# A decoder block on one core: weight tiles all at one place within 512 bytes, 64 bytes past four token operands and level with three

## The chip, the core and the metric

The kernel runs on one core of one Trainium2 chip. The metric is the device time of one execution in microseconds (us): 2169.51 us for the kernel before, the median of three runs (2157.59, 2169.51 and 2170.23).

## The reference, cut to what matters

One layer of a hybrid decoder block on 512 tokens of width 2048, all in float32. First comes token mixing (gated linear attention and differential softmax attention side by side, with one input and one output projection), then a gated MLP with a short causal convolution on its gate branch. Each part has a norm before and a norm after it and is added to the residual.

```python
def conv_ffn(h, w_ffn_in, conv_w, conv_b, w_ffn_out):
    up = h @ w_ffn_in                      # 512x2048 @ 2048x11264
    a, b = up[..., :D_FF], up[..., D_FF:]  # D_FF = 5632
    a = ...                                # causal convolution of width 3, plus conv_b
    return (jax.nn.gelu(a, approximate=True) * b) @ w_ffn_out

def reference(x, ...):
    h = rmsnorm(x, attn_pre_norm[l])
    m = token_mixer(h, ...)                # ends with  o @ w_o
    x = x + rmsnorm(m, attn_post_norm[l])
    h = rmsnorm(x, ffn_pre_norm[l])
    f = conv_ffn(h, ...)
    x = x + rmsnorm(f, ffn_post_norm[l])
```

## The kernel before, in words

**Arithmetic.** Every large product is made of three matmuls. A value is split into a high part, which ScalarE writes (L130 for weights), and a low part, the rest, which VectorE writes (L131); the three products are high by high, low by high and high by low. A weight tile ("granule") has 128 partitions by 1024 values. It is loaded into `raw` or `rt` and split into the tiles `whi` and `wlo`, of which the pool `w` has three buffers each. Tokens that were split lie in the two large tiles `ah` and `al`.

**Stages.** The input projections and the attention come first. The output projection `w_o` follows, with `evac_m` (L625 to L629) taking each finished bank: ScalarE squares it for the norm (L627, its output goes to a scratch tile `jk5`), VectorE multiplies it by the gain (L629). `to_ffn`, whose order is written by hand, turns the result into tokens for the MLP; there the matmuls of the first weights of `w_ffn_in` run on 256 tokens at a time with weights in spare tiles `xhi` and `xlo`, or in `whi` and `wlo`. Then comes the **up stage**: 20 units (ten groups of columns, two branches), each a seven-product scheme in place of eight block products. The class `Unit` runs the seven segments x0, z0, y0, z1, x1, y1, y2. A segment takes two granules. Its token operand is one of a11, a12, a22, s7, which are quarters of `ah` and `al`, or one of the three sums s5, s2, s3, which have tiles of their own (`s5h`, `s5l` and so on). In `up_prods` (L920 to L922) a matmul streams 256 tokens, two blocks of 128 values, against 128 by 128 weights: 24 matmuls a granule, 48 a segment, 336 a unit. When a group is done, `token_sums` makes the sums of its results for the stage after, in VectorE additions (L988) into tiles of tag `sum`, each stored to DRAM by a DMA that SyncE issues. Last comes the **down stage** with the same scheme: in `down_prods` (L1017 to L1019) a matmul streams 512 weight columns against 128 by 128 tokens.

**Places in SBUF.** The tile framework gives the addresses. In the built program `ah`, `al`, the six tiles of the sums, and `xhi` and `xlo` all start at 256 modulo 512 bytes, and every block of 128 values that a matmul reads of them starts there too. A buffer of `whi` or `wlo` is `GR + 64` values long, 4352 bytes, which is eight and a half times 512, so that neighbouring buffers alternate: `whi` starts at 256, 0, 256 modulo 512 and `wlo` at 0, 256, 0. Where `place_w[0]` is 16, the 1024 values begin 16 values (64 bytes) into the buffer, at 320 or 64. That is so in all segments of the up stage, where `self.a == 4`, and for the `whi` and `wlo` of `w_ffn_in` in `to_ffn`. Elsewhere it is 0. The matmul's stationary operand is loaded by its own instruction (LDWEIGHTS, PEld in the profile), which runs while the matmul before it still streams.

**Order.** Outside of the parts ordered by hand, the framework's scheduler sets each engine's order, and each engine takes its instructions in that order. A tile that is taken from a pool waits until the last use of the buffer's earlier tile is over, its DMA included.

Of the kernel before, what the change touches and what calls it, by code (L numbers as in the profile page):

```python
# [9 lines left out]
F32 = mybir.dt.float32  # L10
F32R = mybir.dt.float32r
U8 = mybir.dt.uint8
AF = mybir.ActivationFunctionType
# [4 lines left out]
P = 128  # L18
# [12 lines left out]
GR = 1024  # L31
# [4 lines left out]
def hybrid_layer(ctx: ExitStack, tc: tile.TileContext, x, attn_pre_norm, w_in, w_alpha_up, b_alpha,  # L36
# [10 lines left out]
    def dma(o, i):  # L47
        return nc.sync.dma_start(out=o, in_=i)
# [3 lines left out]
    act = nc.scalar.activation  # L52
# [22 lines left out]
    wpool = ctx.enter_context(tc.tile_pool(name="w", bufs=3))  # L75
# [30 lines left out]
    place_w = [0]  # L106

    def halves():
        sl = slice(place_w[0], place_w[0] + GR)
        return [wpool.tile([P, GR + 64], F32R, name=n, tag=n)[:, sl] for n in ("whi", "wlo")]  # L110

    kept = []

# [7 lines left out]
    def granule(src, a, raw=None, spare=None, hl=None):  # L121
        if raw is None:
            raw = load(src, a)
        if hl is not None:
            hi, lo = hl[:, 0, :], hl[:, 1, :]
        elif spare:
            hi, lo = spare_halves(spare)
        else:
            hi, lo = halves()
        act(hi, raw, AF.Copy)  # L130
        tt(lo, raw, hi.bitcast(F32), ALU.subtract)  # L131
        r = "p (a b) -> p a b"
        return hi.rearrange(r, a=a), lo.rearrange(r, a=a)
# [182 lines left out]
    for li, hs in enumerate(LEVELS):  # L316
        nb = 64 // hs
        m = setup[:, 1024 + 64 * li:1024 + 64 * (li + 1)]
# [298 lines left out]
    wp = wo.enter_context(tc.tile_pool(name="wo", bufs=1))  # L617
    m = [wp.tile([P, D], F32, name=f"m{t}") for t in range(NT)]
# [4 lines left out]
    ssm = [few.tile([P, 4], F32, name=f"ssm{t}") for t in range(NT)]  # L623

    def evac_m(c, t, b):  # L625
        jk = wp.tile([P, 512], F32, name="jk5", tag="jk5", bufs=1)
        act(jk, b, AF.Square, accum_out=ssm[t][:, c:c + 1])  # L627
        sl = slice(512 * c, 512 * (c + 1))
        tt(m[t][:, sl], b, g1[:, sl], ALU.mult)  # L629

    order = [(s + 8) % 16 for s in range(KT)]
    for c in range(3):
        proj_n(w_o3, 512 * c, lambda t, b, c=c: evac_m(c, t, b), order)
# [3 lines left out]
    def to_ffn():  # L637
# [10 lines left out]
        def evac(t):  # L648
            xr[t] = wp.tile([P, D], F32, name="xr", tag="xr", bufs=2)
            dma(xr[t], x2[t * P:(t + 1) * P, :])  # L650
            evac_m(3, t, banks[t])
            ss = small.tile([P, 1], F32, name="ss", tag="ss")
            nc.vector.reduce_sum(ss, ssm[t], axis=AX.X)
            rs[t] = rsqrt_mean(ss, D)
# [94 lines left out]
    fp = ctx.enter_context(tc.tile_pool(name="fp", bufs=2))  # L749
# [102 lines left out]
    class Unit:  # L852
# [4 lines left out]
        def run(self, seg, op, raws):  # L857
            c = seg[0]
            if seg[1] == "0":
                self.banks[c] = self.chain(c)  # L860
            for g in range(2):
                turn[0] += 1
                place_w[0] = 16 if self.a == 4 else 0
                hl = granule(None, self.a, raws[g], spare=extra[0] and turn[0] % 4 == 0)
                self.prods(self.banks[c], op, g, hl, seg[1] == "0")

# [111 lines left out]
    def token_sums(gi, u0, u1):  # L978
        c, i = (gi - 1) // 2, (gi - 1) % 2
        T = [slice(0, 256), slice(256, 512)]  # L980
        a11, a21, a12, a22 = u0[:, :, T[0]], u0[:, :, T[1]], u1[:, :, T[0]], u1[:, :, T[1]]

        def put(n, src):
            dma(sd[c][n][:, i, :].rearrange("p (n t) -> p n t", n=2), src)

        def add(n, x, y, op):
            t = fp.tile([P, 2, 256], F32, name=n, tag="sum", bufs=3)
            tt(t, x, y, op)  # L988
            put(n, t)
            return t  # L990

        put("a11", a11)
        put("a12", a12)
        put("a22", a22)
        s5 = add("s5", a21, a22, ALU.subtract)
        s2 = add("s2", s5, a11, ALU.subtract)
        add("s7", a11, a21, ALU.subtract)
        add("s3", s2, a12, ALU.add)
# [222 lines left out]
```

## Time and profile before

| | |
|---|---|
| median of three runs | 2169.51 us (2157.59 to 2170.23) |
| the profiled execution's own time | 2165.04 us |
| its span, first to last instruction | 2163.3 us |
| TensorE busy | 2133.1 us, 99% |
| VectorE, ScalarE, GpSimd busy | 1418.1, 901.7, 204.9 us |
| granted TensorE clock, mean | 0.998 of 2.4 GHz |

Busy time of an engine is the time covered by its instructions. Matmuls overlap one another in these records (one of 256 columns lasts 281 ns, and the next starts long before it ends), so what a matmul costs in a dense stream is read from the distance between the starts of neighbours, and not from its duration. "Idle before, releaser" says what an engine waited for.

### The profile page before, as it was taken

To read this page: it belongs to the slowest core of one execution; us is meant where nothing else is said; L and a number is where in the kernel's file an instruction comes from. 1 tells how busy PE (TensorE), PEld (TensorE's weight loads), DVE (VectorE), ACT (ScalarE), POOL (GpSimd) and SP (SyncE) were. 2 spreads that over 40 slices of the span, in tenths; PEclk is the share of its full clock that TensorE was granted. 3 is DMA by queue.
4 is the path that set the end of the run, shared out by engine and by line. 5 is a ranking of instruction groups with operands and counts; after the bars stand their busy time and mean duration, and the time that the engine had idled before them with its cause. 6 is when DMAs were issued, how large, how long until landed. Compare 5 with 4: busy or idle time off the path is not lost.

```text
span 2163.3 us, 31876 instructions
## 1 busy us (share of the span) xinstructions
PE 2133.1 (99%) x13009; PEld 1902.4 (88%) x13009; DVE 1418.1 (66%) x1722; ACT 901.7 (42%) x1162; POOL 204.9 (9%) x245
## 2 busy tenths in 40 slices
PE   7999999999999999999999999999999999999997
PEld 6878888888888889899999999999999978887886
DVE  5345553444444236787777677786777787888987
ACT  4233332333333234344444444543544555443533
POOL 1000000000000000011101101111111011111101
PEclk9999999999999999999999999999999999999999
DMA  6322222223224344455666657657667688577663
GB/s 212 104 69 78 78 73 84 69 78 87 78 88 166 98 136 170 132 127 136 161 163 154 159 147 180 157 129 184 147 143 184 182 243 217 166 193 177 158 173 136
DMA packets 218472, 303.83 MB, mean 140 GB/s; under 512 B 11777, under 2 KB 155573, under 8 KB 216405
## 3 DMA queue, kind: packets, MB, share of 16 engines
q1 hardware_dynamic: 165204, 238.87, 33.1%
q0 software_dynamic: 53120, 62.92, 18.9%
q8 instruction: 102, 1.67, 0.3%
q14 instruction: 46, 0.37, 0.0%
HBM read 273.97 MB, written 27.79 MB: 139 GB/s over the span
## 4 chain that ended last, share of the span: by engine, by line
PE 62%; issue 29%; POOL 3%; DVE 2%; DMA 2%; ACT 1%; SPq 0%; POOLq 0%; DVEq 0%; ACTq 0%
PE bank L184 6%; PE bank L185 6%; PE bank L186 6%; PE bank L920 5%; PE bank L922 5%; PE bank L921 5%; PE bank L168 5%; PE bank L166 5%; PE bank L167 5%; PE bank L1018 2%; PE bank L1019 2%; PE bank L1017 2%; POOL rt L869 1%; POOL raw L869 1%; PE bank L434 1%
## 5 line engine op out<-in xcount | busy, mean ns | idle before, releaser
L131 DVE TENSOR_TENSOR wlo<-raw,whi 128x1024 fp32r<-128x1024 f32 x307 | 374.3, 1221 | 360.4 <-ACT whi L130 352.6
L130 ACT ACTIVATE whi<-raw 128x1024 fp32r<-128x1024 f32 x307 | 324.9, 1059 | 599.1 <-PE bank L186 158.0
L922 PE MATMUL bank<-ah,wlo 128*128 128x256 f32 x1280 | 359.4, 281 | 0.6 <-DVE wlo L131 0.6
L920 PE MATMUL bank<-ah,whi 128*128 128x256 f32 x1280 | 359.2, 281 | 0.0
L921 PE MATMUL bank<-al,whi 128*128 128x256 f32 x1280 | 359.2, 281 | 0.0
L131 DVE TENSOR_TENSOR wlo<-rt,whi 128x1024 fp32r<-128x1024 f32 x221 | 269.1, 1221 | 105.2 <-ACT whi L130 105.1
L130 ACT ACTIVATE whi<-rt 128x1024 fp32r<-128x1024 f32 x221 | 233.3, 1059 | 241.2 <-PE bank L921 177.7
L922 PEld LDWEIGHTS bank<-ah,wlo 128*128 128x128 f32 x1280 | 242.9, 190 | 0.9 <-DVE wlo L131 0.8
L921 PEld LDWEIGHTS bank<-al,whi 128*128 128x128 f32 x1280 | 242.7, 190 | 0.1
L920 PEld LDWEIGHTS bank<-ah,whi 128*128 128x128 f32 x1280 | 240.3, 188 | 0.1
L184 PE MATMUL bank<-whi,ah 128*128 128x512 f32 x600 | 236.6, 397 | 0.5 <-ACT ah L143 0.5
L185 PE MATMUL bank<-wlo,ah 128*128 128x512 f32 x600 | 235.5, 393 | 0.0
L186 PE MATMUL bank<-whi,al 128*128 128x512 f32 x600 | 234.7, 393 | 0.0
L166 PE MATMUL bank<-ah,whi 128*128 128x512 f32 (+1 forms) x512 | 196.0, 383 | 0.0
L168 PE MATMUL bank<-ah,wlo 128*128 128x512 f32 (+1 forms) x512 | 194.6, 380 | 0.0
L167 PE MATMUL bank<-al,whi 128*128 128x512 f32 (+1 forms) x512 | 194.4, 380 | 0.0
L1018 PE MATMUL bank<-wlo,ah 128*128 128x512 f32 x424 | 166.2, 392 | 1.2 <-DVE wlo L131 1.1
L1019 PE MATMUL bank<-whi,al 128*128 128x512 f32 x424 | 165.7, 391 | 0.0
L1017 PE MATMUL bank<-whi,ah 128*128 128x512 f32 x424 | 156.7, 391 | 2.7 <-ACT whi L130 2.4
L186 PEld LDWEIGHTS bank<-whi,al 128*128 128x128 f32 x600 | 113.1, 188 | 24.2 <-DVE al L144 0.3
L185 PEld LDWEIGHTS bank<-wlo,ah 128*128 128x128 f32 x600 | 113.1, 189 | 23.7 <-DVE wlo L131 0.5
L184 PEld LDWEIGHTS bank<-whi,ah 128*128 128x128 f32 x600 | 113.0, 189 | 23.7 <-ACT ah L143 0.9
(259 smaller groups left out, 4080.0 us busy)
## 6 DMA issues: line engine op xcount, KB each, us to landing
raw<-in_w_in_dram SPq DMA_DIRECT2D x96, 512.0 KB, 3.7
raw<-in_w_ffn_in_dram SPq DMA_DIRECT2D x96, 512.0 KB, 4.6
raw<-in_w_ffn_out_dram SPq DMA_DIRECT2D x48, 512.0 KB, 6.2
rt<-in_w_ffn_in_dram SPq DMA_DIRECT2D x40, 512.0 KB, 5.6
rt<-in_w_ffn_in_dram POOLq DMA_DIRECT2D x40, 512.0 KB, 6.2
raw<-in_w_ffn_in_dram POOLq DMA_DIRECT2D x40, 512.0 KB, 7.1
raw<-in_w_o_dram SPq DMA_DIRECT2D x32, 512.0 KB, 3.8
rt<-in_w_ffn_out_dram SPq DMA_DIRECT2D x20, 512.0 KB, 6.3
```

What stands on the lines that cost most here:

```text
L130: act(hi, raw, AF.Copy)
L131: tt(lo, raw, hi.bitcast(F32), ALU.subtract)
L166: mm(o, wh, ah[:, t0:t1, kk, :], start=st, stop=False)
L167: mm(o, wh, al[:, t0:t1, kk, :], start=False, stop=False)
L168: mm(o, wl, ah[:, t0:t1, kk, :], start=False, stop=sp)
L184: mm(banks[t], ah[:, t, s, :], w[0][:, k, :], start=st, stop=False)
L185: mm(banks[t], ah[:, t, s, :], w[1][:, k, :], start=False, stop=False)
L186: mm(banks[t], al[:, t, s, :], w[0][:, k, :], start=False, stop=sp)
L920: mm(o, wh, sh[:, :, kk, :], start=start and kk == 0 and n == 0, stop=False, **NOW)
L921: mm(o, wh, sl[:, :, kk, :], start=False, stop=False, **NOW)
L922: mm(o, wl, sh[:, :, kk, :], start=False, stop=kk == HK - 1, **NOW)
L1018: mm(b[j], sh[:, o:o + P], w[1][:, q, :], start=False, stop=False, **NOW)
```

## The change

The diff has three parts. The buffers of `whi` and `wlo` become `GR + 128` values long, 4608 bytes, nine times 512, so that all six start at 256 modulo 512. In the up stage the 64 bytes are kept for the four operands that lie in `ah` and `al`, and are dropped for the three sums. To make room (the six buffers take 1536 bytes more per partition), `evac_m` loses its scratch tile, and its square is written to the place in `m` that the next instruction overwrites; and the tag `sum` has two buffers in place of three.

```diff
-        return [wpool.tile([P, GR + 64], F32R, name=n, tag=n)[:, sl] for n in ("whi", "wlo")]
+        return [wpool.tile([P, GR + 128], F32R, name=n, tag=n)[:, sl] for n in ("whi", "wlo")]
...
     def evac_m(c, t, b):
-        jk = wp.tile([P, 512], F32, name="jk5", tag="jk5", bufs=1)
-        act(jk, b, AF.Square, accum_out=ssm[t][:, c:c + 1])
         sl = slice(512 * c, 512 * (c + 1))
+        act(m[t][:, sl], b, AF.Square, accum_out=ssm[t][:, c:c + 1])
         tt(m[t][:, sl], b, g1[:, sl], ALU.mult)
...
-                place_w[0] = 16 if self.a == 4 else 0
+                place_w[0] = 16 if self.a == 4 and op in ("a11", "a12", "a22", "s7") else 0
...
-            t = fp.tile([P, 2, 256], F32, name=n, tag="sum", bufs=3)
+            t = fp.tile([P, 2, 256], F32, name=n, tag="sum", bufs=2)
```

Where each operand starts, modulo 512 bytes, by the addresses of the two built programs:

| matmuls | token operand | weights before | weights after |
|---|---|---|---|
| up stage, a11, a12, a22, s7 | 256 | 320 or 64 | 320 |
| up stage, s5, s2, s3 | 256 | 320 or 64 | 256 |
| `to_ffn`, `whi` and `wlo` of `w_ffn_in` | 256 | 320 or 64 | 320 |
| `to_ffn`, `xhi` and `xlo` | 256 | 256 | 256 |
| all other stages | 256 | 256 or 0 | 256 |

No other tile changes its place modulo 512.

VectorE's order around the token sums, group 2, from the addition that makes s2 on. Before:

```order
L988 TENSOR_TENSOR s_8848<-s_8845,u 128x512 [waits DVE_49]
L988 TENSOR_TENSOR s_8851<-u 128x512
L131 TENSOR_TENSOR wlo<-raw,whi 128x1024 [waits PE_49,Activation_49]
L988 TENSOR_TENSOR s_8854<-s_8848,u 128x512 [waits DMAHW6_49,DVE_49]
L946 SCALAR_TENSOR_TENSOR u<-bank,p_8857 128x2x256 [waits PE_49]
L131 TENSOR_TENSOR wlo<-raw,whi 128x1024 [waits Activation_49]
L131 TENSOR_TENSOR wlo<-raw,whi 128x1024 [waits PE_49,Activation_49]
L948 TENSOR_TENSOR u<-u,bank 128x2x256 [waits DVE_49,PE_49]
```

The four rows of L988 of a group are s5, s2, s7, s3 in this order; the first stands above this piece. With the change:

```order
L987 TENSOR_TENSOR s_8832<-s_8829,u 128x512 [waits DVE_49]
L131 TENSOR_TENSOR wlo<-raw,whi 128x1024 [waits PE_49,Activation_49]
L987 TENSOR_TENSOR s_8835<-u 128x512 [waits DMAHW6_49,DVE_49]
L945 SCALAR_TENSOR_TENSOR u<-bank,p_8841 128x2x256 [waits PE_49]
L131 TENSOR_TENSOR wlo<-raw,whi 128x1024 [waits Activation_49]
L131 TENSOR_TENSOR wlo<-raw,whi 128x1024 [waits PE_49,Activation_49]
L987 TENSOR_TENSOR s_8838<-s_8832,u 128x512 [waits DMAHW0_49,DVE_49]
L947 TENSOR_TENSOR u<-u,bank 128x2x256 [waits DVE_49,PE_49]
```

s7 moved behind one weight split and now waits for a DMA, that of s5, whose buffer it takes. s3 moved behind two more weight splits and waits for the DMA of s2 instead of that of s5.

SyncE's order at the same place, before:

```order
L48 DMA sd0s_6677<-s_8848 128x512 [waits DMAHW7_49,DVE_49]
L48 DMA sd0s_6678<-s_8851 128x512 [waits DMAHW0_49,DVE_49]
L48 DMA sd0s_6679<-s_8854 128x512 [waits DMAHW1_49,DVE_49]
L48 DMA raw<-in_w_ffn_in_dram 128x4x256 [waits DMAHW2_49,DVE_49]
L48 DMA raw<-in_w_ffn_in_dram 128x4x256 [waits DMAHW3_49,DVE_49]
L48 DMA raw<-in_w_ffn_in_dram 128x4x256 [waits DMAHW4_49,DMASW2_49,DVE_49]
```

With the change:

```order
L48 DMA sd0s_6661<-s_8832 128x512 [waits DMAHW7_49,DVE_49]
L48 DMA sd0s_6662<-s_8835 128x512 [waits DMAHW0_49,DVE_49]
L48 DMA raw<-in_w_ffn_in_dram 128x4x256 [waits DMAHW1_49,DVE_49]
L48 DMA raw<-in_w_ffn_in_dram 128x4x256 [waits DMAHW2_49,DVE_49]
L48 DMA sd0s_6663<-s_8838 128x512 [waits DMAHW3_49,DVE_49]
L48 DMA raw<-in_w_ffn_in_dram 128x4x256 [waits DMAHW4_49,DMASW2_49,DVE_49]
```

The store of s3 moved behind two weight loads; nothing else changed its place.

## Rows read from the trace of the kernel before

**Rows 1.** The page: busy time of the engines over the whole span.

```profile
PE 2133.1 (99%) x13009; PEld 1902.4 (88%) x13009; DVE 1418.1 (66%) x1722; ACT 901.7 (42%) x1162; POOL 204.9 (9%) x245
```

**Rows 2.** Busy time by window: the up stage.

```profile
core 0: us, PE busy (x) PEld busy (x) DVE busy (x) ACT busy (x) POOL busy (x), PEclk, DMA share, GB/s
926.90:1723.20 796.30, 795.71 (x6746) 794.19 (x6744) 596.47 (x603) 375.15 (x409) 102.57 (x80) 1.00 0.67 158
```

**Rows 3.** Waits of TensorE in 927 to 1723 us (total, times, longest).

```profile
PE bank L922 <- DVE wlo L131: 0.6, 1, 0.6
```

**Rows 4.** Matmuls of the up stage by line (count, busy, mean ns, idle before).

```profile
L920 PE MATMUL bank<-ah,whi 128*128 128x256 f32 x1280 | 359.2, 281 | 0.0
...
L920 PE MATMUL bank<-s5h,whi 128*128 128x256 f32 x320 | 89.8, 281 | 0.0
...
L1018 PE MATMUL bank<-wlo,ah 128*128 128x512 f32 x8 | 3.1, 391 | 0.0
```

**Rows 5.** Timeline of TensorE in the up stage: segments y0 and z1, start and duration.

```profile
1096.70 0.28 PE L920 MATMUL bank<-s2h,whi 128*128 128x256 f32 x1
1096.82 0.28 PE L921 MATMUL bank<-s2l,whi 128*128 128x256 f32 x1
...
1102.36 0.28 PE L920 MATMUL bank<-s3h,whi 128*128 128x256 f32 x1
...
1105.65 0.28 PE L922 MATMUL bank<-s3h,wlo 128*128 128x256 f32 x1
```

**Rows 6.** The same view in `to_ffn`, weights in the spare tiles.

```profile
866.38 0.28 PE L166 MATMUL bank<-ah,xhi 128*128 128x256 f32 x1
866.50 0.28 PE L167 MATMUL bank<-al,xhi 128*128 128x256 f32 x1
866.62 0.28 PE L168 MATMUL bank<-ah,xlo 128*128 128x256 f32 x1
...
877.78 0.28 PE L168 MATMUL bank<-ah,xlo 128*128 128x256 f32 x1
```

**Rows 7.** Matmuls by line in exactly that stretch.

```profile
L166 PE MATMUL bank<-ah,xhi 128*128 128x256 f32 x32 | 9.1, 283 | 0.0
L167 PE MATMUL bank<-al,xhi 128*128 128x256 f32 x32 | 9.1, 283 | 0.0
L168 PE MATMUL bank<-ah,xlo 128*128 128x256 f32 x32 | 9.1, 283 | 0.0
```

**Rows 8.** Timeline of TensorE in the down stage.

```profile
1800.19 0.39 PE L1019 MATMUL bank<-whi,al 128*128 128x512 f32 x1
1800.42 0.39 PE L1017 MATMUL bank<-whi,ah 128*128 128x512 f32 x1
...
1813.11 0.39 PE L1019 MATMUL bank<-whi,al 128*128 128x512 f32 x1
```

**Rows 9.** One line: the square in `evac_m`, and who waited for it.

```profile
L627 ACT ACTIVATE jk<-bank x16: 597/598/601, 695.3 to 833.7; 128x512 f32<-128x512 f32 x16
...
  DVE m L629: 9.3, 11
```

**Rows 10.** Timeline of VectorE at the token sums of group 2.

```profile
1096.94 0.68 DVE L988 TENSOR_TENSOR s<-u 128x512 f32<-128x512 f32 x1
...
1100.41 0.68 DVE L988 TENSOR_TENSOR s<-s,u 128x512 f32<-128x512 f32 x1
1101.01 0.68 DVE L988 TENSOR_TENSOR s<-u 128x512 f32<-128x512 f32 x1
1101.62 1.22 DVE L131 TENSOR_TENSOR wlo<-raw,whi 128x1024 fp32r<-128x1024 f32 x1
1102.75 0.69 DVE L988 TENSOR_TENSOR s<-s,u 128x512 f32<-128x512 f32 x1
...
1106.36 1.22 DVE L131 TENSOR_TENSOR wlo<-raw,whi 128x1024 fp32r<-128x1024 f32 x1 [1.19 <-ACT whi L130]
```

**Rows 11.** Landing of the stores of sums: groups 1 and 2, then 9 and 10.

```profile
DMA to landing us min/median/max: 2.0/2.3/5.3
...
DMA to landing us min/median/max: 2.7/5.0/10.2
```

## The prediction

> **What bounds the kernel now.** The first view is the page's busy time: TensorE is busy for 2133.1 us of 2163.3, and VectorE, the next engine, for 1418.1 [rows 1]. So a change gains or loses only through the time that TensorE needs, or through a new wait of TensorE for one of the others. The second view is the window of the up stage, the only stage where the change alters a place at which nothing of the kind stood before: 796.3 us long, TensorE busy for 795.7 of them at a granted clock of 1.00, which is 2.4 GHz [rows 2]. The third is TensorE's waits there: one, of 0.6 us [rows 3]. Nothing in this stage hides behind anything else; a nanosecond more per matmul is paid in full. VectorE is idle there for 200 us of the 796 and can take some delay.
>
> The fourth view is the distance between starts of matmuls, since their durations overlap. The up stage has 6720 matmuls of 256 columns (1280 on each of three lines for `ah` and `al`, 320 on each of three lines for each of the three sums) and 26 of 512 that the scheduler drew in [rows 2, 4]. A matmul of 512 columns takes 0.2267 us: in the down stage 57 steps take 1813.11 - 1800.19 = 12.92 us [rows 8]. That leaves (796.3 - 26 x 0.227 - 0.6) / 6720 = **117.5 ns** for a matmul of 256 columns. One look inside agrees roughly: from the first matmul of s2 to the first of s3 there are 48 steps, 1102.36 - 1096.70 = 5.66 us, or 117.9 ns [rows 5]. Weights stand there 64 bytes past their tokens, or 320 bytes past, modulo 512.
>
> The fifth view is the same kind of matmul with weights level with the tokens, which the kernel before has in one place: `to_ffn` with `xhi` and `xlo`, both operands at 256 modulo 512. There 96 matmuls [rows 7] start at 866.38 to 877.78, 95 steps in 11.40 us: **120.0 ns** each [rows 6], with no wait. The number of columns, the split and the clock are those of the up stage; what differs is the place of the weights, and the tiles themselves.
>
> **The change, part by part.**
>
> *The three sums, weights now level.* Nine groups of 320 matmuls (three lines by three sums) are 2880 [rows 4]. No row shows this operand with level weights. From one side, the nearest row is the level stretch at 120.0 ns [rows 6]: 2880 x (120.0 - 117.5) = +7.2 us. From the other, the cheapest row per column is half of a 512-column matmul, 113.4 ns [rows 8], which has weights level with tokens in part of that stretch: 2880 x (113.4 - 117.5) = -11.8 us. I take the first, since it agrees with the up stage in the columns of a matmul, in the operand that streams and in the split, while the second streams weights and not tokens and spreads its fixed part over twice the columns. The sums' two blocks lie 4096 bytes apart and those of `ah` 8192; both are multiples of 512, so the same collision, if it is one of places within 512 bytes, should be met. Upward, the far bound would be a weight load that is no longer hidden at all; I keep it as a small chance only.
>
> Here the Trainium skill speaks against any effect: its page "TensorE: Matmul & The Clock Gate", section "Part 2: What happens when you issue a matmul", says that TensorE reads SBUF through two independent ports, so that loading the next weights takes no bandwidth from the running matmul. By that rule this term is 0 and the sum stays at 2165.0 us. The two stretches of 117.5 and 120.0 ns do not agree with it, but they differ in tiles too.
>
> *The four operands in `ah` and `al`.* Weights were at 64 or 320 past the tokens, two buffers in three at one and the third at the other, and the change leaves them all at 64. Both kinds were mixed in the 117.5 ns, and within the 48 steps of s2 high parts stood at one and low parts at the other, without neighbours standing apart [rows 5]. I cost it at 0.
>
> *All other stages.* Weights were level or 256 bytes off, and are level now. The 57 steps of the down stage go through tiles of both kinds, and every step between neighbours is 0.22 or 0.23 us [rows 8]. The cost is 0.
>
> *The scratch tile of `evac_m`.* Writing the square into `m` makes the multiplication wait for the square. It does so already: the multiplication sat idle until the square had ended 11 times in 16 [rows 9], because both read one bank. No wait is added: 0.
>
> *Two tiles for sums.* Each of ten groups gets a new wait on VectorE: s7 for the store of s5, s3 for the store of s2. In group 2, s5 is made by 1096.94 + 0.68 = 1097.62 us, and s7 now comes behind the split that started at 1101.62, some 0.6 us earlier than there since s7 no longer stands ahead of it: at about 1102.2, 4.6 us after s5. s3 comes behind the split of 1106.36, at about 1107.6, 6.5 us after s2 was made at 1101.1 [rows 10]. Stores of sums land 2.3 us after their issue in the middle and 5.3 at most in groups 1 and 2; in groups 9 and 10, where transfers are denser, 5.0 and 10.2 [rows 11]. So mostly the store is over when its buffer is wanted. Where one is late, the wait holds up VectorE, and behind it the weight splits; TensorE feels it only once the lead of the splits is used up. The split of 1101.62 ends at 1102.84, and its low part is first read at 1105.65 [rows 5, 10]: a lead of 2.8 us. The worst store seen, 10.2 us, would cost 10.2 - 6.5 - 2.8 = 0.9 us. I take 0 and keep up to 10 x 0.9 = 9 us for the range. The moved addition itself (0.68 us) falls into the 1.19 us that VectorE waited for ScalarE [rows 10]. The store of s3 moves behind two weight loads on SyncE, and its reader comes in the down stage, far later; the two loads gain a place.
>
> **Sum.** The profiled execution took 2165.04 us, 1.7 more than its span. 2165.0 + 7.2 = **2172.2 us**. The median of the three runs is 4.5 us above the profiled execution; on it the same sum would be 2176.7, inside the range.
>
> **Rivals.**
>
> - *Level weights cost nothing with the sums*: the 120.0 ns belong to the spare tiles or to `to_ffn`, or the load of weights disturbs no stream at any place. For it: level weights cost nothing in the 512-column stages [rows 8]. Against it: 95 steps without a single wait, 2 % dearer than the same matmul elsewhere. Time: 2165.0 us.
> - *Level is the better place for the sums.* For it: the cheapest columns in the trace include level ones [rows 8]. Against it: the only level matmuls of 256 columns are the dearest. Time: down to 2165.0 - 11.8 = 2153.2 us, 2159 at half of it.
> - *The wait for stores of sums reaches TensorE.* Place: s3 on VectorE in the ten groups. It decides from a landing of 6.5 + 2.8 = 9.3 us. For it: one store took 10.2 us [rows 11], and the stage moves 158 GB/s [rows 2]. Against it: the middle value is 2.3 to 5.0 us. Price: with landings of 12 us in all groups, 10 x 2.7 = 27 us, so 2172.2 + 27 = 2199 us, slower than before by 1.6 %.
> - *Level weights hit the sums much harder than `ah`*: slower by over 1 % from (21.7 + 2880 x 0.1175) / 2880 = 125.0 ns a matmul on. No row shows so much.
>
> **How the numbers follow.** Chances: the forecast 0.58; no cost of level weights 0.23; level better 0.11; the wait for stores 0.05; much harder 0.03. One measurement of this kernel can tell about 1 % from no change, some 22 us. The forecast (+0.3 %), the first rival and all of the second that has a price lie within 1 %. Faster by over 1 % has no priced case; I leave 0.03 for it, out of "level better". Slower by over 1 % has 0.06 from the last two rivals and the bound of the stores. Within 1 % is 0.91. The range goes from 2156 us (most of "level better", or the first rival at the lower run of before, 2157.59) to 2184 us (the forecast on the higher run, 2170.23 + 7.2 = 2177.4, and most of the 9 us for late stores).
>
> **What would show it.** Right: in the up stage the matmuls of s5, s2 and s3 start 120 ns apart, and those of `ah` and `al` still 117.5; the up stage is about 7 us longer; TensorE's waits in it stay below some us; `evac_m` and the 512-column stages are as before. Wrong: the sums still at 117.5 (first rival) or below it (second), or idle time of VectorE at L987 put down to a store, with TensorE waiting for `wlo` behind it (third).

## The result: 7.5 us slower, as forecast

The changed kernel takes **2176.62 us** (median of 15 runs), the kernel before 2169.16 us in the same session (15 runs): a ratio of 1.004, 95% interval 1.0031 to 1.0048. The profiled execution took 2175.78 us, with a span of 2174.1. Two slow runs in the session of experiments 1, 2, 3 and 5 (8214.58 us of experiment 1's kernel, 7592.79 us of the kernel before) stand in the medians given there and are left out of the ratios.

The page after, the line that answers to [rows 1], and the window of the up stage, which answers to [rows 2] (columns as there):

```profile
PE 2142.4 (99%) x13009; PEld 1909.3 (88%) x13009; DVE 1418.8 (65%) x1722; ACT 901.1 (41%) x1162; POOL 204.8 (9%) x245
```

```profile
927.40:1731.10 803.70, 803.66 (x6746) 802.34 (x6744) 598.75 (x604) 376.80 (x410) 102.50 (x80) 1.00 0.66 156
```

TensorE works 9.3 us longer; VectorE and ScalarE do what they did. The up stage grew from 796.3 to 803.7 us at the same clock of 1.00, with the same 6746 matmuls, and TensorE is busy in all of it: nothing is waited for. From first to last matmul of 256 columns the stage takes 796.0 us before and 803.3 after, **+7.3 us**. So the matmuls themselves got dearer. Which ones, the view by line shows, beside [rows 4] (count, busy, mean ns):

```profile
L919 PE MATMUL bank<-ah,whi 128*128 128x256 f32 x1280 | 359.7, 281 | 0.0
...
L919 PE MATMUL bank<-s2h,whi 128*128 128x256 f32 x320 | 90.6, 283 | 0.0
```

The four operands in `ah` and `al` keep their 281 ns; the sums went from 281 to 283. What one costs is read from starts. The timeline of TensorE in the same segments as [rows 5] (start, duration); the rows are the first matmul of s2, the first of s3, the first of x1, and the 46th of x1:

```profile
1098.49 0.28 PE L919 MATMUL bank<-s2h,whi 128*128 128x256 f32 x1
...
1104.25 0.28 PE L919 MATMUL bank<-s3h,whi 128*128 128x256 f32 x1
...
1110.01 0.28 PE L919 MATMUL bank<-ah,whi 128*128 128x256 f32 x1
...
1115.31 0.28 PE L919 MATMUL bank<-ah,whi 128*128 128x256 f32 x1
```

s2 and s3 take 48 steps in 5.76 us each, **120.0 ns** a matmul. Then x1, whose operand lies in `ah`, takes 45 steps in 5.30 us, **117.8 ns**. Before, the 48 steps of s2 took 5.66 us [rows 5].

The two cheap parts of the change show as follows. The multiplication in `evac_m` waits for the square as often as in [rows 9], now by another name:

```profile
  ACT m L627: 9.0, 11
```

And the two tiles for sums do make VectorE wait for a store, in group 4 for instance (timeline of VectorE; in brackets the idle time before a row and what ended it; the rows of L987 are s7 and s3):

```profile
1263.39 0.68 DVE L987 TENSOR_TENSOR s<-u 128x512 f32<-128x512 f32 x1
...
1267.86 1.23 DVE L131 TENSOR_TENSOR wlo<-raw,whi 128x1024 fp32r<-128x1024 f32 x1 [1.66 <-ACT whi L130]
1269.36 0.69 DVE L987 TENSOR_TENSOR s<-s,u 128x512 f32<-128x512 f32 x1 [0.28 <-DMA sd1s<-s]
```

VectorE sits idle in front of s3 in groups 1 to 9: 0.2 to 0.75 us in the seven groups where the trace names a store, at most 0.1 us in the other two. None of it reaches TensorE in the up stage. The store that s3 waits for is that of s7: in group 4 it landed at 1269.27 us, just ahead of s3's start.

### The profile page after: what moved, and what is told of

Its sections match the earlier page's. It is cut to its first block, busy times and chain, and to the rows that moved or that the text cites. A ratio compares the mean times of both kernels' runs of the same rounds, so it can differ in the third digit from the quotient of the medians.

```text
span 2174.1 us, 31863 instructions
## 1 busy us (share of the span) xinstructions
PE 2142.4 (99%) x13009; PEld 1909.3 (88%) x13009; DVE 1418.8 (65%) x1722; ACT 901.1 (41%) x1162; POOL 204.8 (9%) x245
## 4 chain that ended last, share of the span: by engine, by line
PE 81%; issue 13%; DVE 2%; DMA 1%; POOL 1%; ACT 1%; SPq 0%; POOLq 0%; DVEq 0%; ACTq 0%
PE bank L920 12%; PE bank L919 12%; PE bank L921 12%; PE bank L184 6%; PE bank L185 6%; PE bank L186 6%; PE bank L168 5%; PE bank L166 5%; PE bank L167 5%; PE bank L434 1%; PE bank L1017 1%; PE bank L1018 1%; PE bank L1016 1%; PE bank L502 1%; PE bank L533 1%
## 5 line engine op out<-in xcount | busy, mean ns | idle before, releaser
L131 DVE TENSOR_TENSOR wlo<-rt,whi 128x1024 fp32r<-128x1024 f32 x221 | 269.1, 1221 | 115.6 <-ACT whi L130 115.5
L185 PEld LDWEIGHTS bank<-wlo,ah 128*128 128x128 f32 x600 | 113.3, 189 | 23.7 <-DVE wlo L131 0.5
```

The lines of the kernel that those rows point to most:

```text
L185: mm(banks[t], ah[:, t, s, :], w[1][:, k, :], start=False, stop=False)
```

## The experiments

Each kernel is the changed one with the edit shown, unless its text says otherwise. "Place" is how many bytes modulo 512 the weights stand past their tokens. Distances of starts are means over all neighbours of a kind in the trace. One detail of the order matters from experiment 3 on: the first segment x0 of a unit runs ahead of the last segment y2 of the unit before.

**1. All seven operands at 64 bytes**: the level place of the sums undone, the rest of the change kept.

```diff
-                place_w[0] = 16 if self.a == 4 and op in ("a11", "a12", "a22", "s7") else 0
+                place_w[0] = 16 if self.a == 4 else 0
```

> The changed kernel, but in the up stage the weights of all seven operands stand 64 bytes past the tokens, those of the three sums too. If level weights are the whole cost: the three sums back from 120.0 to 117.5 ns a matmul, up stage 796 us instead of 803.3, median 2169 (before 2169.2, the change 2176.6). If the cost lies in the rest of the change (longer buffers, two tiles for sums, no scratch tile): the sums still at 120, median 2176 to 2177.

Measured: 2167.96 us, ratio to before 0.9993 (0.9972 to 1.0014). From the first matmul of s2 to the first of s3 in the same segments:

```profile
1097.02 0.28 PE L919 MATMUL bank<-s2h,whi 128*128 128x256 f32 x1
...
1102.67 0.28 PE L919 MATMUL bank<-s3h,whi 128*128 128x256 f32 x1
```

48 steps in 5.65 us, 117.7 ns (117.8 over the whole stage). The level place alone made the kernel slower; putting it back gives everything back.

**2. The places swapped**: `ah` and `al` level, the sums at 64 bytes.

```diff
-                place_w[0] = 16 if self.a == 4 and op in ("a11", "a12", "a22", "s7") else 0
+                place_w[0] = 16 if self.a == 4 and op in ("s5", "s2", "s3") else 0
```

> The changed kernel with the two places swapped: weights level with the four operands in ah and al, 64 bytes past the three sums. If place alone decides, whatever the tile: 3840 matmuls at 120.0 ns and 2880 at 117.5, so 3840 x 2.45 = 9.4 us over the kernel before, median 2178.6, up stage 805. If it is something about the tiles of the sums: ah and al stay at 117.5, median 2169, up stage 796.

Measured: 2174.77 us, ratio 1.0038 (1.0024 to 1.0052). Timeline of TensorE; the first matmuls of s2, of s3 and of x1, and the 115th from there:

```profile
1098.82 0.28 PE L919 MATMUL bank<-s2h,whi 128*128 128x256 f32 x1
...
1104.47 0.28 PE L919 MATMUL bank<-s3h,whi 128*128 128x256 f32 x1
...
1110.13 0.28 PE L919 MATMUL bank<-ah,whi 128*128 128x256 f32 x1
...
1123.81 0.28 PE L919 MATMUL bank<-ah,whi 128*128 128x256 f32 x1
```

Now s2 runs at 5.65 / 48 = 117.7 ns and `ah` at 13.68 / 114 = 120.0. The place decides, whichever tile holds the tokens. The up stage is 8.5 us longer than with experiment 5's weights (805.3 against 796.8), as 3840 x 2.2 ns make it.

**3. A sweep of places**: another place in each of the 20 units of the up stage and the ten of the down stage.

```diff
+    offs = {4: [0, 1, 2, 4, 6, 8, 12, 16, 20, 24, 32, 40, 48, 64, 80, 96, 112, 120, 124, 127],
+            2: [0, 2, 4, 8, 16, 32, 64, 96, 112, 124]}
...
+            self.off = offs[a].pop(0)
...
-                place_w[0] = 16 if self.a == 4 and op in ("a11", "a12", "a22", "s7") else 0
+                place_w[0] = self.off
```

> The changed kernel with another place of the weights in each unit: in the 20 units of the up stage 0, 4, 8, 16, 24, 32, 48, 64, 80, 96, 128, 160, 192, 256, 320, 384, 448, 480, 496 and 508 bytes past the tokens, in the 10 of the down stage 0, 8, 16, 32, 64, 128, 256, 384, 448 and 496. If only the exact level collides: 120.0 ns in the first unit and 117.5 in the 19 others. If nearness counts: a slope from 120 to 117.5 within the first units and again in the last. If half of 512 is bad as well, the unit at 256 is at 120. Down stage: 226.7 ns in every unit if 512 columns never mind, and lower than that somewhere if level and 256 were both bad places there.

Measured: 2175.19 us in one run. Mean distance by place, in ns: in the up stage (256 columns) over the five segments z0 to y1 of a unit, 240 matmuls each; in the down stage (512 columns) over some 100 or more, without stalls and without weights in the spare tiles:

```
up    0:120.0   4:118.3   8:115.6  16:118.3  24:121.9  32:118.4  48:117.8
     64:113.3  80:118.8  96:118.7 128:120.0 160:120.0 192:117.8 256:120.0
    320:117.8 384:118.6 448:117.8 480:117.8 496:120.0 508:120.0
down  0:227.1   8:232.9  16:231.6  32:233.3  64:229.4 128:233.2 256:227.5
    384:233.3 448:233.2 496:233.3
```

Two things came out that no theory here had. The 64 bytes that ran at 117.8 ns in all of experiment 1 run at 113.3 here. The same happened within two units: at 192 and at 320 bytes the five segments ran at 117.8, but y2, behind the first segment of the next unit, at 113.3 and 113.8. And with 512 columns the level place is the best one, with 256 bytes beside it.

**4. Only the sums' tiles moved**, to 256, 64, 0, 448, 384 and 320 modulo 512, with high and low weights each at its own tile's place; in every second unit 64 bytes past it.

```diff
+    at = {"s5": (0, 80), "s2": (64, 48), "s3": (32, 16)}
+    by = [0, 16] * 10
...
+                    hi, lo = at.get(op, (0, 0))
+                    place_w[:] = [hi + self.more_by, lo + self.more_by]
...
-        return fp.tile([P, D], dt, name=name, tag="t8", bufs=6)
+        return fp.tile([P, D + 16], dt, name=name, tag="t8", bufs=6)[:, :D]
```

> The changed kernel with the six tiles of the sums moved to 256, 64, 0, 448, 384 and 320 modulo 512, and the high and the low weights moved with them, each to the place of the tokens that stream while they are loaded. In every other unit all weights stand 64 bytes further. If only the distance between weights and tokens counts: in the level units 120.0 ns a matmul for each sum, at three different places, and for ah and al (level too), and in the other units 117.8 or 113.3. If what is bad is the place 256 itself, as in the kernel so far: s2 and s3, whose weights are not at 256, at 117.8 in the level units too, and only s5, ah and al at 120.

Measured: 2177.35 us in one run. In level units the sums ran at 117.9 (s5), 119.6 (s2) and 119.6 (s3), `ah` at 120.0; in the units at 64 bytes at 118.4, 119.2 and 118.8, `ah` at 117.8. s2 and s3 are near what a rule by distance asks for in the level units, but s5, which both theories put at 120.0, is not, and in the other units no sum is at 117.8 or 113.3. With high and low tiles at different places the pattern of a segment is no longer uniform. Whether distance alone counts stays open.

**5. The other two edits alone**: the kernel before, with the scratch tile gone and two tiles for sums.

```diff
-        jk = wp.tile([P, 512], F32, name="jk5", tag="jk5", bufs=1)
-        act(jk, b, AF.Square, accum_out=ssm[t][:, c:c + 1])
+        act(m[t][:, sl], b, AF.Square, accum_out=ssm[t][:, c:c + 1])
...
-            t = fp.tile([P, 2, 256], F32, name=n, tag="sum", bufs=3)
+            t = fp.tile([P, 2, 256], F32, name=n, tag="sum", bufs=2)
```

> The kernel before with only the two edits that make room: two tiles for sums instead of three, and no scratch tile in evac_m; all weights stand as before. If these cost nothing: 2169, the up stage 796 us with all matmuls at 117.5. If the waits of VectorE for the stores reach TensorE: up to 9 us more, with waits of TensorE for wlo in the up stage.

Measured: 2167.70 us against 2167.18, ratio 1.001 (0.9995 to 1.0025). They cost nothing that this can tell. With the weights where they stood before, the trace has all matmuls of 256 columns at 117.8 ns, no stall among them, and an up stage of 796.8 us.

**6. Kicks**: 64 bytes had two speeds, so what went before must matter. In each unit the first granule is level, the second stands at a "kick" place, and all later ones at a base of 64, 192 or 320 bytes. Between the kick and the rest runs y2 of the unit before, at that unit's base.

```diff
+            self.kick, self.base = kicks.pop(0) if a == 4 else (0, 0)
...
+                if self.a == 4:
+                    place_w[0] = (0, self.kick)[g] if seg == "x0" else self.base
```

> Theory: at 64 bytes the stream of matmuls has two steady states, 117.8 and 113.3 ns a matmul, and what comes just before decides which one; level weights have one, 120.0. So in each unit the first granule is level (which led to 117.8 every time so far), the second stands at a place of its own (4 to 496 bytes in the first 14 units, other pairs in the last 6), and the other six segments at 64 (then 192 and 320) bytes. If a place just before sets the state: 113.3 in the segments after some of the places, 48 bytes among them, and 117.8 after the others, the unit with no second place among these; where 113.3 is reached it holds to the unit's end. Rival: the states come from stalls and drift and not from the place before, so that there is no relation to the second granule, and 117.8 nearly everywhere.

Measured: 2156.34 us in one run, against 2167.81. Distance in the rest of a unit, by base and kick (bytes):

```
base  64: 113.3 after 24, 40, 56, 96, 496
          117.8 after 8, 16, 32, 48, 64, 80, 128, 256, 384
base 192: 113.3 after 192, 256, 48
base 320: 113.3 after 320; 117.8 after 384, 48
```

So there are **two steady distances for the same matmuls at the same place**, and whichever was entered lasts until something breaks it. Which kick leads to which has no rule that I can see, and each pair was tried once. The unit "320 after 320" came from a unit at 192 that ran at 113.3 in five segments; y2 of that unit, behind the kick, ran at 117.7.

**7, 8 and 9. Versions made from that.** In 7 everything stands at 192 bytes, and the first granule of each unit is level; in 8 only the first granule of the whole stage is. In 9 everything stands at 64 bytes and the first granule of each unit at 96 (its expectation says both granules; the kernel places only the first there).

```diff
7  +                place_w[0] = 48 if self.a == 4 and not (seg == "x0" and g == 0) else 0
8  +                place_w[0] = 48 if self.a == 4 and not (seg == "x0" and g == 0 and self.first) else 0
9  +                place_w[0] = (16 if seg != "x0" or g else 24) if self.a == 4 else 0
```

> All seven operands of the up stage take weights 192 bytes past their tokens, but each unit's first granule lies level. Theory of steady distances between matmuls (120.0 ns level; 113.3 ns at 192 bytes when a level granule came before): 20 level granules of 24 matmuls, some 0.5 thousand, at 120.0, the other 6240 at 113.3, so against the kernel before, whose steady distance is 117.8, the up stage falls by 6240 x 4.45 - 480 x 2.2 = 26.7 us, to about 769 us, and the time to about 2142. Rival, the next engine in line takes over: VectorE or ScalarE can't feed TensorE at 113.3 ns, waits show in the up stage, and the time stays above 2150. Rival, the quick stretches of the earlier trials were luck: some units run at 117.8 and the time lies between 2150 and 2168.

> The same, but only the very first granule of the up stage lies level. If the steady distance holds through everything that follows, all units run at 113.3 ns and the time is about 1 us under that of the kernel that goes level in each unit, some 2141. If a stall of TensorE throws it back to 117.8, the stage is quick up to the first stall and then like before, up to 2168.

> All seven operands at 64 bytes, each unit's first segment entered with two granules... the second of x0 as the rest, the first segment of a unit at 96 bytes in both granules and 64 after it, with no level granule. Theory: from 96 bytes the 64-byte matmuls go on at 113.3 ns, as they did in one unit of the earlier trial, where a level granule came first; the segment itself runs at some 118.8. Gain against before about 20 x 276 x 4.45 = 24.6 us, to about 2145. If the level granule was what counted, all stays at 117.8 and the time is that of the kernel with 64 bytes everywhere, 2168.

Measured against 2166.48 us for the kernel before: 7 takes **2144.00 us**, ratio 0.9890 (0.9873 to 0.9906); 8 takes 2166.67 us, 1.0002 (0.9993 to 1.0012); 9 takes **2141.64 us**, 0.9889 (0.9872 to 0.9905). Timeline of TensorE in kernel 7, from s3 on into x1:

```profile
1025.85 0.28 PE L919 MATMUL bank<-s3h,whi 128*128 128x256 f32 x1
...
1031.63 0.28 PE L919 MATMUL bank<-ah,whi 128*128 128x256 f32 x1
```

51 steps in 5.78 us, 113.3 ns. Kernel 8 had this too, until a stall at 942 us:

```profile
941.40 0.28 PE L923 MATMUL bank<-s2h,whi 128*128 128x256 f32 x1
...
941.74 0.28 PE L923 MATMUL bank<-s2h,whi 128*128 128x256 f32 x1
...
941.96 0.28 PE L923 MATMUL bank<-s3h,whi 128*128 128x256 f32 x1
942.08 0.28 PE L924 MATMUL bank<-s3l,whi 128*128 128x256 f32 x1
942.32 0.39 PE L925 MATMUL bank<-s2h,wlo 128*128 128x256 f32 x1
942.55 0.28 PE L923 MATMUL bank<-s2h,whi 128*128 128x256 f32 x1
...
942.90 0.28 PE L923 MATMUL bank<-s2h,whi 128*128 128x256 f32 x1
```

Three steps take 0.34 us ahead of the stall (two steps of 0.24 and 0.23) and 0.35 behind it. To the hundredth that is little; over the 40 steps from 946.8 us on it is 117.8 ns, and it stays so to the end of the stage at 1725 us. Kernel 7 is thrown back by a stall of the same size at the same place. The level granule of its second unit, at 961 us, does not help; that of the third, at 1002 to 1004 us, brings 113.3 ns again. It fails once more at 1116 us and is mended by the next at 1157. So a level granule leads to the quick distance mostly, not always; returning it in each unit is all that sets 7 apart from 8, and it is worth 22 us. Kernel 9 differs from experiment 1's in the granules at 96 bytes alone. They brought the quick distance in every unit, but the first unit lost it to a stall at the same place. The rival that VectorE could not feed TensorE at this speed fell: in kernel 7 all waits of TensorE in the stage come to 0.3 us (total, times, longest):

```profile
PE bank L921 <- DVE wlo L131: 0.3, 1, 0.3
```

The stage of kernel 7 takes 775.1 us, 6 more than expected. The two lost stretches, some 820 matmuls x 4.45 ns, are 3.6 of them; stalls are 1.2; and 0.8 come from the start of that sum, 796.0 us with a quick stretch in it, where experiment 5 has 796.8 without one.

**10. The same hunt in the down stage**: kernel 7, with a pair of kick and base in each down unit.

```diff
+    kicks = [(48, 48), (64, 48), (24, 16), (14, 16), (64, 80), (12, 16), (48, 64), (16, 64), (48, 0), (24, 0)]
...
+                else:
+                    place_w[0] = (0, self.kick)[g] if seg == "x0" else self.base
```

> The kernel with 192 bytes and a level granule per unit in the up stage, and in the down stage (512 moving columns) another pair of places in each of the ten units: the first granule level, the second at one place, all later segments at another: 192 after 192, 192 after 256, 64 after 96, 64 after 56, 320 after 256, 64 after 48, 256 after 192, 256 after 64, level after 192, level after 96 bytes. Theory that the steady distance between matmuls has a quick value here too, as for 256 columns (where it lay 6.7 ns under that of the level place): some units run at 220.0 instead of 226.7 ns, which is 57 steps of a granule x 14 granules x 6.7 ns = 5 us in a unit. Rival, level is already the quick value of this form: no unit under 226.7 ns, those off it at 229 to 233 ns, and the time 5 to 10 us above the kernel with level weights there.

Measured: 2146.30 us in one run. Level 227.0 ns, 256 bytes 227.1, 64 and 320 bytes 229.5, 192 bytes 233.3: no quick value, the rival held. With 512 columns level is right. (A granule of the down stage has 12 matmuls, not the 57 of the expectation, so even a quick value would have been worth 168 x 6.7 ns = 1.1 us in a unit.) The up stage, which is that of kernel 7, adds something: at 943 us it has a stall of 0.25 us like the one that threw kernel 7 back, and here the distance is 113.3 ns behind it too.

**11 and 12. Both kernels again**, unchanged, for a second trace.

> The kernel before, unchanged, a second trace. If the quick stretch of the first trace (some 480 matmuls 113.3 ns apart between a stall and the next) comes from stalls that differ from one execution to the next, it is at another place, longer, shorter or missing here, and the up stage takes 797.5 us (none; as the kernel with 64 bytes everywhere) minus 4.45 ns for each matmul in it. If it belongs to the program, the stage again takes 796.0 us with the stretch at 1298 to 1352 us.

> The changed kernel, unchanged, a second trace. The sums 120.0 ns apart again and ah and al at 117.8, an up stage within 1 us of 803.3. The 3.1 us that the first trace showed behind the up stage, beside the kernel before, are waits there that differ between executions: if so they are partly gone here; if they belong to the program (two tiles for sums, later stores), they come back.

Measured, one run each: 2160.96 us (before) and 2171.11 us (changed). The second trace of the kernel before has a quick stretch at another place and nearly twice as long. It begins behind a step of 0.15 us and ends at one of 0.31 (timeline of TensorE):

```profile
1355.71 0.28 PE L921 MATMUL bank<-al,whi 128*128 128x256 f32 x1
1355.83 0.31 PE L922 MATMUL bank<-ah,wlo 128*128 128x256 f32 x1
1355.98 0.28 PE L920 MATMUL bank<-ah,whi 128*128 128x256 f32 x1
...
1356.33 0.28 PE L920 MATMUL bank<-ah,whi 128*128 128x256 f32 x1
...
1357.35 0.28 PE L920 MATMUL bank<-ah,whi 128*128 128x256 f32 x1
...
1453.95 0.28 PE L921 MATMUL bank<-s2l,whi 128*128 128x256 f32 x1
1454.26 0.39 PE L922 MATMUL bank<-s2h,wlo 128*128 128x256 f32 x1
```

1356.33 to 1357.35 is nine steps in 1.02 us, 113.3 ns. The up stage took 793.6 us, 2.4 less than in the first trace. The changed kernel repeats: sums at 120.0, `ah` and `al` at 117.8, an up stage of 803.2 us. What follows its up stage took 426.6 us here and 430.7 in its first trace, 424.2 and 427.6 in the kernel before: the spread within a kernel is as large as the difference.

## Why the prediction was right, and where a step of it was not

- **The bound.** Right: what a matmul of the up stage costs is paid in full. +7.3 us in the stage, +7.5 us in the medians. The two profiled executions are 10.7 us apart, but 3.1 of these lie behind the up stage, where two traces of one kernel differ as much.
- **The level sums.** Sized 2880 x (120.0 - 117.5) = 7.2 us. The 120.0 ns taken from `to_ffn` [rows 6] held to the digit, and experiments 1 and 2 show that it is the place. But the 117.5 was a mean of two things. Nearly all of the up stage before runs at 117.8 ns, and one stretch at 113.3. Its middle, in the timeline of the kernel before:

```profile
1297.72 0.28 PE L921 MATMUL bank<-s2l,whi 128*128 128x256 f32 x1
1297.97 0.38 PE L922 MATMUL bank<-s2h,wlo 128*128 128x256 f32 x1
...
1319.97 0.28 PE L920 MATMUL bank<-ah,whi 128*128 128x256 f32 x1
...
1325.75 0.28 PE L920 MATMUL bank<-ah,whi 128*128 128x256 f32 x1
...
1352.38 0.28 PE L921 MATMUL bank<-al,whi 128*128 128x256 f32 x1
1353.25 0.38 PE L922 MATMUL bank<-ah,wlo 128*128 128x256 f32 x1 [0.59 <-DVE wlo L131]
```

  1319.97 to 1325.75 is 51 steps in 5.78 us, 113.3 ns; a step of 0.25 us begins the stretch and a wait of 0.59 ends it. So the term is 2880 x 2.2 = 6.4 us, and the rest up to 7.3 is that stretch, some 476 matmuls x 4.45 ns = 2.1 us, which the changed kernel doesn't have, less the 1.3 us of stalls that the kernel before had in the stage. The sum came out right in part because the mean that it used had the stretch in it. That the sum on the median, 2176.7, is met to 0.1 us is luck: what stretches the untraced executions had is not known. The check offered for it (117.9 ns in one segment) was the steady value, and a warning: two readings that should agree and differ by 0.4 ns over 6720 matmuls differ by 2.7 us.
- **`ah` and `al` at 0.** Right for the steady value: 117.8 ns with the mixed places of before (experiment 5) and with 64 bytes throughout (experiment 1). The quick stretch is what this step missed: it shows in neither trace of the changed kernel. It does not show in the traces of experiments 1 and 5 either, which have no level place in the up stage. None of these four has a stall ahead of 1718 us that could begin one. So that the return to level prevents it is not shown.
- **The rival that level costs nothing**, with the rule that it rested on (the Trainium skill, "TensorE: Matmul & The Clock Gate", section "Part 2: What happens when you issue a matmul": loading the next weights takes no bandwidth from the running matmul), fell: by it the changed kernel and that of experiment 2 would be at before's time, and both are slower by the 2.2 ns a matmul that the place sets. The measurement decides. Level as the better place fell with it; and in the 512-column stages, from which that rival drew its price, level is indeed best (experiments 3 and 10).
- **The wait for stores.** Right at 0, with one detail wrong: s3 was said to wait for the store of s2, 6.5 us old. s3 reads s2's tile, so it takes s7's buffer and waits for s7's store, which took 4.9 to 5.4 us in the four groups whose landing the trace has. VectorE waited for it in seven groups of ten, at most 0.75 us. The lead of the weight splits covered all of it; experiment 5 gives nothing outside the interval.
- **`evac_m` and other stages at 0.** Right as far as two traces of each kernel can tell.

## What to carry to other kernels

In a stage that TensorE bounds, take the distance of starts over each stretch apart before using its mean: 0.3 ns over 6720 matmuls is 2 us, and a mean can hide a state that some other place of the weights would make permanent. The place of weights against tokens within 512 bytes is a knob worth a sweep for each number of moving columns, since the best place for 256 (192 or 64 bytes, entered again and again from another place: 1.1% of this kernel) is not the best for 512 (level).

## What the runs showed of the hardware that was not expected

- The distance of matmuls of 256 columns, two tokens' blocks against one weight tile, took three steady values at level and at 64, 192 and 320 bytes: 113.3, 117.8 and 120.0 ns. Level gave 120.0 always; the other three gave 113.3 or 117.8, by what came before. Some other places of the sweep gave values of their own, from 115.6 at 8 bytes to 121.9 at 24.
- The weight loads carry a trace of it, which does not explain it. In level stretches of the changed kernel every load lasts 192 ns; in the kernel before, at 117.8 ns, one load in three lasts 192 and two 188; in its quick stretch all last 188. But in kernel 7, at 192 bytes, all last 188 at either distance.
- A state outlives segments and changes of weight tiles (some 860 matmuls in the second trace of the kernel before, and whole units in kernels 6, 7 and 9). In the traces of the kernel before it began and ended at stalls of TensorE of 0.03 to 0.75 us; a stall of 0.25 us at 1432 us in the second of them did neither. The size of a stall does not decide: 0.25 us near 942 us ended it in kernels 7 and 8 and not in kernel 10.
- What in the chip makes this is open: the runs show that the distance and the history set it, and no trace shows the reads themselves.
